# The later modulation sums without a seed page: the bias is added where the sums are used

## The chip, the cores and the metric

One core of a Trainium2 chip runs one transformer block in a single launch. The time is the device time of an execution in microseconds (us), as the median of several. The core's engines are TensorE (PE in the profile, with its weight loads as PEld), VectorE (DVE), ScalarE (ACT), GpSimd (POOL) and SyncE (SP). Each has an instruction queue of its own; SP's queue issues nearly all DMA transfers.

## The reference, cut to what matters

```python
mod = jax.nn.silu(c) @ w_mod[layer] + b_mod[layer]            # 1 x 12288
sh_m, sc_m, g_m, sh_f, sc_f, g_f = jnp.split(mod[:, None, :], 6, axis=-1)
h_lat = rms_norm(x, nw[0]) * (1.0 + sc_m) + sh_m              # and the same for 256 context tokens
m_ctx, m_lat = hybrid_mixer(h_ctx, h_lat, ...)                # gated LRU and gated delta net, w_in, w_out
x = x + g_m * rms_norm(m_lat, nw[1])
h = rms_norm(x, nw[2]) * (1.0 + sc_f) + sh_f
x = x + g_f * rms_norm(sq_relu_mlp(h, w_ff1, w_ff2), nw[3])
```

The model has 2048 columns, 512 tokens (and 256 context tokens), and an inner width of 8192 in the last product. The modulation `mod` has six chunks of 2048 columns: 0 and 1 are needed at the start, 2 (`g_m`) behind the mixer, 3 and 4 (`sh_f`, `sc_f`) ahead of the last product, and 5 (`g_f`) at the very end. Everything is 32-bit; the large products are made of pairs of rounded pieces (high times high, high times low, low times high), so each weight piece is split into a high part `wh` (a cast on ScalarE) and a low part `wl` (a subtraction on VectorE or GpSimd, `split`, line 67 and 61) before TensorE multiplies it.

## The kernel before, in words

The program runs in stages. First comes the modulation's chunks 0 and 1, by matmuls. Then the mix stage: the product with `w_in`, and between its tiles the tasks of the mixer, which a planner in the source hands out in slots. Then the product with `w_out` (`project`), and then the last product, block by block: `ff1(b)` multiplies by a 512-column block of `w_ff1` (16 weight pieces), `ff2(b)` by the matching rows of `w_ff2` (four quarters of four pieces, with four additions on VectorE behind each quarter). The order is ff1_half for blocks 0 and 1, ff2(0), ff1(2), ff2(1), ff1(3), ff2(2), ff1(4), and so on. Three buffers each hold raw weights (`wr`), high parts and low parts, so that about three pieces are split ahead of TensorE.

Chunks 2 to 5 of the modulation are running sums. `modacc` (line 1144) takes one quarter of a chunk, 512 columns: it loads sixteen 128 x 512 slices of `w_mod` into the five pages of the tag `ld` and accumulates each on VectorE, times one column of silu(c) (`stt`, line 64). Partition p then holds the sum over sixteen of the 2048 rows, and a matmul with a matrix of ones later adds the partitions up. The bias enters through a seed: a page of the tag `macc`, which has one buffer, is cleared on GpSimd (line 1148), the bias row is loaded into its partition 0 (line 1149), and the first accumulate adds this page. In chunks 2 to 4 the sum itself is kept in a PSUM bank and copied to the seed page at the end (line 1164); in chunk 5 the seed page is the sum. The page is stored to `accD` in memory (line 1165).

The sums are read back where they are used: `gm_rows` (chunk 2, line 1292) and `modrow` (chunk 5, line 1181) multiply by the ones matrix to have the row on all partitions; `mod_vecs` (chunks 3 and 4, line 1308) makes columns of it. The call of chunk 5 stands in the source behind ff2(2): sixty-four accumulates, and then `modrow`'s four matmuls ahead of ff1(4). Its accumulates carry a manual order edge to an earlier VectorE instruction (`after`).

A scheduler in the framework gives each engine its final queue at compile time. It takes instructions in the order of the source as a priority, but an instruction may go far ahead of that place if its inputs and its buffer are there. Buffers of one tag are handed out in the order of the source. Pages of the common tag (`pg`) are a pool of 29; tags such as `macc` and `ld` have buffers of their own.

The two strict triangle masks GT and LT are made on GpSimd (line 77) and copied to rounded forms GTr and LTr on ScalarE (lines 89 and 90).

Of the kernel before, what the change touches and what calls it, by code (L numbers as in the profile page):

```python
# [7 lines left out]
F32 = mybir.dt.float32  # L8
# [3 lines left out]
ALU = mybir.AluOpType  # L12
# [4 lines left out]
P = 128  # L17
# [14 lines left out]
def build(tc, A, out, stop=None, dump=None):  # L32
# [3 lines left out]
    with es:  # L36
        cp = es.enter_context(tc.tile_pool(name="const", bufs=1))
        wp = es.enter_context(tc.tile_pool(name="weights", bufs=2))
        pp = es.enter_context(tc.tile_pool(name="pages", bufs=29))
        ld_n = 5  # L40

        pg = ps = es.enter_context(tc.tile_pool(name="psum", bufs=8, space=PSUM))
# [7 lines left out]
        def page(dt=F32, tag="pg", shape=(P, 512), bufs=None):  # L50
            kw = {} if bufs is None else {"bufs": bufs}
            return pp.tile(list(shape), dt, tag=tag, name=nm(tag), **kw)
# [22 lines left out]
        def select(name, op, mult, patt, dt=F32):  # L75
            t = const([P, P], dt, name)
            G.affine_select(out=t, in_=ones, compare_op=op, fill=0.0, base=0,
                            pattern=[[patt, P]], channel_multiplier=mult)
            return t
# [2 lines left out]
                        pattern=[[-1, P]], channel_multiplier=1)  # L82
        LE = select("LE", ALU.is_ge, -1, 1)
        GE = select("GE", ALU.is_ge, 1, -1)
        GT = select("GT", ALU.is_gt, 1, -1)
        LT = select("LT", ALU.is_gt, -1, 1)
        GTr = const([P, P], F32R, "GTr")
        LTr = const([P, P], F32R, "LTr")
        S.copy(GTr, GT)
        S.copy(LTr, LT)  # L90
        sel = const([4, 2], F32, "sel")
        G.affine_select(out=sel, in_=ones[:4, :2], compare_op=ALU.is_ge, fill=0.0, base=0,
                        pattern=[[-2, 2]], channel_multiplier=1)
# [1050 lines left out]
        def modacc(chunk, f, after=None):  # L1144

            col = chunk * D + f * 512
            acc = seed = page(tag="macc", bufs=1)
            G.memset(acc, 0.0)
            SP.dma_start(acc[0:1, :], A["b_mod"][:, col:col + 512])
            if after is None:  # L1150
                acc = bank()
            q = []
            for k in range(17):
                if k < 16:
                    w = page(tag="ld", bufs=ld_n)
                    SP.dma_start(w, wmod[:, k, col:col + 512])
                    q.append(w)
                if k > 0:
                    stt(acc, q.pop(0), silc[:, k - 1:k], seed if k == 1 else acc, ALU.mult, ALU.add)
                    if after is not None:  # L1160
                        tc.add_manual_dep(nc.cur_bb.bb.instructions[-1], after, NOSYNC, reason="order")
                    yield 0.7, 0, 0
            if after is None:
                S.copy(seed, acc)
            SP.dma_start(accD[4 * (chunk - 2) + f], seed)
            modok.add((chunk, f))

        def modload(chunk, f):
            a = page(tag="ld", bufs=ld_n)
# [3 lines left out]
        def modrow(chunk, nrow):  # L1173

            res = []
            for f in range(4):
                a = modload(chunk, f)
                nb = page(tag="ld", bufs=ld_n)
                SP.dma_start(nb, A["norm_w"][0, nrow:nrow + 1, f * 512:(f + 1) * 512].to_broadcast([P, 512]))
                b = bank()  # L1180
                T.matmul(b, ones, a, start=True, stop=True)
                g = page()
                tt(V, g, b, nb, ALU.mult)
                res.append(g)
            return res

        def modcol(chunk, dst):
            for f in range(4):
                a = modload(chunk, f)
                b = bank()  # L1190
                for i in range(4):
                    T.matmul(b[:, i:i + 1], a[:, i * P:(i + 1) * P], ones[:, 0:1], start=True, stop=True)
                V.tensor_copy(dst[:, 4 * f:4 * f + 4], b[:, 0:4])


        ORD = "ckcccucc cccccFzc ccculuyu uycuuymu Lgxggggg ggggggyg yzxgyggg xxgyyxxg gggxggzx zzzzz".replace(" ", "")
# [86 lines left out]
        def gm_rows():  # L1283
            while any((2, f) not in modok for f in range(4)):
                yield 0, 0, 1
            for f in range(4):
                a = modload(2, f)
                nb = page(tag="ld", bufs=ld_n)
                SP.dma_start(nb, A["norm_w"][0, 1:2, f * 512:(f + 1) * 512].to_broadcast([P, 512]))
                yield 0, 0, 2  # L1290
                b = bank()
                T.matmul(b, ones, a, start=True, stop=True)
                g = page()
                tt(V, g, b, nb, ALU.mult)
                gm.append(g)
                yield 0.6, 0, 0
# [3 lines left out]
        def mod_vecs():  # L1300
            for ch, dst in ((3, shf), (4, scf)):
                while any((ch, f) not in modok for f in range(4)):
                    yield 0, 0, 1
                a = [modload(ch, f) for f in range(4)]
                yield 0, 0, 2
                b = bank()
                for i in range(16):
                    T.matmul(b[:, i:i + 1], a[i // 4][:, i % 4 * P:i % 4 * P + P], ones[:, 0:1], start=True, stop=True)
                V.tensor_copy(dst, b[:, 0:16])
                del a  # L1310
            stt(scf, scf, 1.0, nw2, ALU.add, ALU.mult)
            colok.append(1)
            yield 0.1, 0, 0
# [280 lines left out]
```

## Time and profile before

| | us |
|---|---|
| runs before (median of 3) | 2782.72 (2778.91 to 2784.66) |
| the profiled execution, its own time | 2792.65 |
| its span, first to last instruction | 2790.9 |
| TensorE busy | 2661.4 (95%) |
| VectorE busy | 1676.4 (60%) |
| ScalarE busy | 1183.7 (42%) |
| GpSimd busy | 585.0 (21%) |

In the profile, a row of a group gives the line, the engine, the operation, the tiles it writes and reads and the count, then the busy time and the mean of one in nanoseconds, then the idle time of the engine right before these instructions with what ended it. A row of the timeline gives the start, the duration and in brackets the idle time before it with its releaser. A row of the waits gives who waited for whom, the sum in us, how often, and the longest. A DMA row gives the size and the median time from issue to landing. Matmuls overlap in the pipeline, so a step from one start to the next says more of their pace than one duration.

### The profile page before, as it was taken

The numbers are of one execution on the slowest core, as the hardware profiler recorded it, in microseconds if no ns is written. First come the engines' busy times: TensorE is split into PE (matmuls) and PEld (weight loads), VectorE is DVE, ScalarE is ACT, GpSimd is POOL, SyncE is SP. The second block draws the span as 40 slices with busy tenths as digits, with TensorE's granted clock in tenths as the row PEclk, the third lists the DMA queues.
The fourth block names the chain that finished last, engine by engine and source line by source line (L and its number), as shares of the span: only waits on it lengthen the run. The fifth ranks groups of instructions, "written<-read, shape, count | busy, mean of one in ns | idle before, by whom it ended". The sixth has DMA issues, their size and how long they took to land.

```text
span 2790.9 us, 39585 instructions
## 1 busy us (share of the span) xinstructions
PE 2661.4 (95%) x14253; PEld 2181.3 (78%) x14253; DVE 1676.4 (60%) x3287; ACT 1183.7 (42%) x2418; POOL 585.0 (21%) x552
## 2 busy tenths in 40 slices
PE   7989999899999998978999999999999999999998
PEld 2478797677877787866898887888888888888886
DVE  6785757877797785857588443344343443434436
ACT  5555577545556654535552222222222222222223
POOL 0145354434344434326300000000000000000002
PEclk9989999999999998989999999999999999999999
DMA  9654475556666676646788333333233333333334
GB/s 355 208 164 127 115 202 166 161 168 198 194 197 193 185 216 216 195 143 205 231 268 276 113 94 118 99 98 98 93 97 98 98 98 97 95 97 98 98 99 155
DMA packets 374968, 434.33 MB, mean 156 GB/s; under 512 B 22665, under 2 KB 212450, under 8 KB 374770
## 3 DMA queue, kind: packets, MB, share of 16 engines
q1 hardware_dynamic: 374160, 431.66, 49.7%
q8 instruction: 112, 1.84, 0.3%
q14 instruction: 86, 0.70, 0.1%
q10 hardware_dynamic: 610, 0.13, 0.0%
HBM read 401.31 MB, written 30.41 MB: 155 GB/s over the span
## 4 chain that ended last, share of the span: by engine, by line
PE 69%; DVE 8%; issue 3%; DMA 2%; ACT 2%; POOL 1%; SPq 0%; DVEq 0%; ACTq 0%; POOLq 0%
PE bk L1510 8%; PE bk L1509 8%; PE bk L1508 8%; PE bk L1498 7%; PE bk L1499 7%; PE bk L1497 7%; PE bk L523 3%; PE bk L525 3%; PE bk L524 3%; PE bk L1419 2%; PE bk L1420 2%; PE bk L1418 2%; DVE pg L64 2%; DVE bk L64 1%; DVE pg L61 1%
## 5 line engine op out<-in xcount | busy, mean ns | idle before, releaser
L67 ACT CAST wh<-wr 128x512 fp32r<-128x512 f32 x952 | 583.4, 618 | 1212.8 <-PE bk L1498 446.6
L61 DVE TENSOR_TENSOR wl<-wr,wh 128x512 fp32r<-128x512 f32 x642 | 463.2, 723 | 776.3 <-ACT wh L67 661.0
L61 POOL TENSOR_TENSOR wl<-wr,wh 128x512 fp32r<-128x512 f32 (+1 forms) x310 | 400.9, 1300 | 587.1 <-ACT wh L67 522.8
L1510 PE MATMUL bk<-wl,pg 128*128 128x512 f32 x960 | 374.0, 390 | 0.5 <-DVE wl L61 0.5
L1509 PE MATMUL bk<-wh,pg 128*128 128x512 f32 x960 | 373.9, 390 | 0.0
L1508 PE MATMUL bk<-wh,pg 128*128 128x512 f32 x960 | 373.9, 389 | 0.0
L1497 PE MATMUL bk<-H2h,wh 128*128 128x512 f32 x896 | 349.4, 390 | 0.0
L1498 PE MATMUL bk<-H2l,wh 128*128 128x512 f32 x896 | 349.0, 389 | 0.0
L1499 PE MATMUL bk<-H2h,wl 128*128 128x512 f32 x896 | 349.0, 389 | 0.0
L523 PE MATMUL bk<-Hlh,wh 128*128 128x512 f32 (+1 forms) x784 | 316.1, 403 | 5.4 <-ACT wh L67 5.4
L525 PE MATMUL bk<-Hlh,wl 128*128 128x512 f32 (+1 forms) x784 | 311.4, 397 | 7.6 <-POOL wl L61 7.4
L524 PE MATMUL bk<-Hll,wh 128*128 128x512 f32 (+1 forms) x784 | 309.8, 395 | 0.0
L61 POOL TENSOR_TENSOR big<-big,pg 128x512 f32<-128x512 f32 x9 | 12.0, 1342 | 1245.6 <-ACT pg L1570 1245.6
L1510 PEld LDWEIGHTS bk<-wl,pg 128*128 128x128 f32 x960 | 180.2, 188 | 38.1 <-DVE wl L61 0.9
L1508 PEld LDWEIGHTS bk<-wh,pg 128*128 128x128 f32 x960 | 180.3, 188 | 37.4
L1509 PEld LDWEIGHTS bk<-wh,pg 128*128 128x128 f32 x960 | 180.3, 188 | 37.3
L1497 PEld LDWEIGHTS bk<-H2h,wh 128*128 128x128 f32 x896 | 168.3, 188 | 35.1 <-issue 0.2
L1498 PEld LDWEIGHTS bk<-H2l,wh 128*128 128x128 f32 x896 | 168.3, 188 | 35.1 <-issue 0.2
L1499 PEld LDWEIGHTS bk<-H2h,wl 128*128 128x128 f32 x896 | 168.2, 188 | 34.8
L525 PEld LDWEIGHTS bk<-Hlh,wl 128*128 128x128 f32 (+1 forms) x784 | 148.2, 189 | 45.5 <-POOL wl L61 13.0
L523 PEld LDWEIGHTS bk<-Hlh,wh 128*128 128x128 f32 (+1 forms) x784 | 148.7, 190 | 36.6 <-ACT wh L67 6.6
L524 PEld LDWEIGHTS bk<-Hll,wh 128*128 128x128 f32 (+1 forms) x784 | 148.6, 190 | 29.7
(348 smaller groups left out, 4524.9 us busy)
## 6 DMA issues: line engine op xcount, KB each, us to landing
wr<-in_w_ff SPq DMA_DIRECT2D x272, 512.0 KB, 4.1
wr<-in_w_in SPq DMA_DIRECT2D x144, 512.0 KB, 4.0
ld<-in_w_mod SPq DMA_DIRECT2D x256, 256.0 KB, 4.0
mr<-in_w_mod SPq DMA_DIRECT2D x32, 1024.0 KB, 11.0
wr<-in_w_out SPq DMA_DIRECT2D x64, 512.0 KB, 4.6
pg<-vkD SPq DMA_DIRECT2D x88, 128.0 KB, 4.1
ld<-in_x SPq DMA_DIRECT2D x32, 256.0 KB, 4.8
vkD<-pg SPq DMA_DIRECT2D x24, 256.0 KB
```

Of the source, the lines that this page charges most:

```text
L61: e.tensor_tensor(out=out, in0=a, in1=b, op=op)
L64: V.scalar_tensor_tensor(out=out, in0=a, scalar=s, in1=b, op0=op0, op1=op1)
L67: S.copy(hi, src)
L523: T.matmul(pt[:m, :n], wh, a, start=k == 0, stop=False)
L524: T.matmul(pt[:m, :n], wh, b, start=False, stop=False)
L525: T.matmul(pt[:m, :n], wl, a, start=False, stop=k == 15)
L1497: T.matmul(bk[c], w[kk][0][:, s_], hh, start=k == 0, stop=False)
L1498: T.matmul(bk[c], w[kk][0][:, s_], hl_, start=False, stop=False)
L1499: T.matmul(bk[c], w[kk][1][:, s_], hh, start=False, stop=k == 15)
L1508: T.matmul(o, ah, h, start=k == 0, stop=False)
L1509: T.matmul(o, al, h, start=False, stop=False)
L1510: T.matmul(o, ah, l, start=False, stop=k == 3)
```

## The change

The seed page is gone, and with it its memset, its bias load and the tag `macc`. The first accumulate becomes a plain multiplication by a scalar. The sum is in a PSUM bank as before for chunks 2 to 4 and copied to a page of the common tag; for chunk 5 it is a page of the common tag from the start. The common pool has 30 pages instead of 29.

The bias is added at the use. For chunks 2 and 5, `modbias` loads the bias row into one partition of an `ld` page, and `modsum` adds a second matmul of one row (ones times the bias row) to the same bank. For chunks 3 and 4, the copy out of PSUM becomes an addition of the bias columns that the kernel keeps from its start. The masks GTr and LTr are now one minus the other triangles, made on VectorE, and GT and LT are the same tiles read as plain 32-bit. A function without a caller, `modcol`, is dropped.

```diff
-        pp = es.enter_context(tc.tile_pool(name="pages", bufs=29))
+        pp = es.enter_context(tc.tile_pool(name="pages", bufs=30))
...
-        GT = select("GT", ALU.is_gt, 1, -1)
-        LT = select("LT", ALU.is_gt, -1, 1)
...
-        S.copy(GTr, GT)
-        S.copy(LTr, LT)
+        for m, mr in ((LE, GTr), (GE, LTr)):
+            V.tensor_scalar(out=mr, in0=m, scalar1=-1.0, scalar2=1.0, op0=ALU.mult, op1=ALU.add)
+        GT, LT = GTr.bitcast(F32), LTr.bitcast(F32)
...
         def modacc(chunk, f, after=None):
             col = chunk * D + f * 512
-            acc = seed = page(tag="macc", bufs=1)
-            G.memset(acc, 0.0)
-            SP.dma_start(acc[0:1, :], A["b_mod"][:, col:col + 512])
-            if after is None:
-                acc = bank()
+            acc = page() if after is not None else bank()
...
-                    stt(acc, q.pop(0), silc[:, k - 1:k], seed if k == 1 else acc, ALU.mult, ALU.add)
+                    if k == 1:
+                        V.tensor_scalar_mul(acc, q.pop(0), silc[:, 0:1])
+                    else:
+                        stt(acc, q.pop(0), silc[:, k - 1:k], acc, ALU.mult, ALU.add)
...
             if after is None:
-                S.copy(seed, acc)
-            SP.dma_start(accD[4 * (chunk - 2) + f], seed)
+                acc, w = page(), acc
+                S.copy(acc, w)
+            SP.dma_start(accD[4 * (chunk - 2) + f], acc)
...
+        def modbias(chunk, f):
+            r = page(tag="ld", bufs=ld_n)[0:1, :]
+            SP.dma_start(r, A["b_mod"][:, chunk * D + f * 512:chunk * D + f * 512 + 512])
+            return r
+
+        def modsum(b, a, r):
+            T.matmul(b, ones, a, start=True, stop=False)
+            T.matmul(b, ones[0:1, :], r, start=False, stop=True)
...
-                a = modload(chunk, f)
+                a, r = modload(chunk, f), modbias(chunk, f)
...
-                T.matmul(b, ones, a, start=True, stop=True)
+                modsum(b, a, r)
...
-                V.tensor_copy(dst, b[:, 0:16])
+                tt(V, dst, b[:, 0:16], bmod[:, 16 * ch:16 * ch + 16], ALU.add)
```

The change moves instructions of chunk 5. On VectorE before, its 64 accumulates (`macc`) stand among the splits of ff1_half and ff2(0), from row 2019 of VectorE's queue to row 2160. Here is the end of the last quarter, with the splits `wl` of ff2(0) and ff1(2) around it:

```order
L61 TENSOR_TENSOR wl_16233<-wr_16226,wh_16232 128x512
L64 SCALAR_TENSOR_TENSOR macc_17492<-ld_17527,silc,macc_17492 128x512
L64 SCALAR_TENSOR_TENSOR macc_17492<-ld_17530,silc,macc_17492 128x512
L64 SCALAR_TENSOR_TENSOR macc_17492<-ld_17533,silc,macc_17492 128x512
L61 TENSOR_TENSOR wl_16263<-wr_16260,wh_16262 128x512
L64 SCALAR_TENSOR_TENSOR macc_17492<-ld_17536,silc,macc_17492 128x512
L64 SCALAR_TENSOR_TENSOR macc_17492<-ld_17539,silc,macc_17492 128x512
L61 TENSOR_TENSOR wl_16267<-wr_16260,wh_16266 128x512
L61 TENSOR_TENSOR wl_16297<-wr_16294,wh_16296 128x512
```

The additions of ff2(2) and of `modrow` follow a hundred rows behind, from row 2262 on.

On VectorE now, the accumulates (`pg_17320`, `pg_17370`, `pg_17420`, `pg_17470`, one page for each quarter) begin at row 2172, within the first quarter of ff2(2), and 26 of them stand there between splits and additions. This is the end of ff2(2) (`big` and `S` are its last additions), the start of what follows:

```order
L61 TENSOR_TENSOR wl_17575<-wr_17568,wh_17574 128x512
L61 TENSOR_TENSOR big_15791<-big_15791,bk_17244 128x512
L61 TENSOR_TENSOR big_15793<-big_15793,bk_17245 128x512
L61 TENSOR_TENSOR big_15795<-big_15795,bk_17246 128x512
L61 TENSOR_TENSOR S_15799<-S_15799,bk_17247 128x512
L64 SCALAR_TENSOR_TENSOR pg_17370<-ld_17400,silc,pg_17370 128x512
L61 TENSOR_TENSOR wl_17605<-wr_17602,wh_17604 128x512
L64 SCALAR_TENSOR_TENSOR pg_17370<-ld_17403,silc,pg_17370 128x512
L64 SCALAR_TENSOR_TENSOR pg_17370<-ld_17406,silc,pg_17370 128x512
```

Behind the split `wl_17605` (the third of ff1(4)) 37 accumulates stand in one block, rows 2229 to 2265 of the queue; then come `modrow`'s four additions and only then the next split.

On TensorE the place of chunk 5 is the same in both. Before it has four rows (line 1181) between the last row of ff2(2) (line 1510) and the first of ff1(4) (line 1497). Now (all lines behind the masks' are one or more off):

```order
L1511 MATMUL bk_17247<-wl_17289,pg_16402 128x512
L1174 MATMUL bk_17526<-ld_17520,ones 128x512
L1175 MATMUL bk_17526<-ld_17522,ones 128x512
L1174 MATMUL bk_17537<-ld_17531,ones 128x512
L1175 MATMUL bk_17537<-ld_17533,ones 128x512
L1174 MATMUL bk_17548<-ld_17542,ones 128x512
L1175 MATMUL bk_17548<-ld_17544,ones 128x512
L1174 MATMUL bk_17559<-ld_17553,ones 128x512
L1175 MATMUL bk_17559<-ld_17555,ones 128x512
L1498 MATMUL bk_17564<-H2h_13478,wh_17570 128x512
```

Each of the four matmuls has its one-row matmul for the bias behind it; nothing else moved there. On SP, the loads of `w_mod` for chunk 5 moved with the accumulates, behind the weight loads of ff2(2), and each of the four reads of `accD` has a bias load and a load of `norm_w` beside it. On GpSimd the sixteen memsets are gone and the order of the rest is the same, but for a few rows that changed places with a neighbour. The accumulates of chunks 2 to 4 stand where they stood.

More of the change, by code (lines that the diff above doesn't have):

```diff
@@ L1185, in modrow @@
             return res
[L1187 to L1193, printed above, removed]
         ORD = "ckcccucc cccccFzc ccculuyu uycuuymu Lgxggggg ggggggyg yzxgyggg xxgyyxxg gggxggzx zzzzz".replace(" ", "")
@@ L1286, in gm_rows @@
             for f in range(4):
-                a = modload(2, f)
+                a, r = modload(2, f), modbias(2, f)
                 nb = page(tag="ld", bufs=ld_n)
@@ L1291, in gm_rows @@
                 b = bank()
-                T.matmul(b, ones, a, start=True, stop=True)
+                modsum(b, a, r)
                 g = page()
```

## The prediction

> **What bounds the kernel now.** I read the page first: its engine table, then the waits of TensorE (PE), then the windows around the places that the diff touches (a window row has the stretch, its length, the busy time of PE, PE's weight loads, DVE, ACT and POOL with their instructions, the granted clock, the DMA share, GB/s).
>
> ```profile
> span 2790.9 us, 39585 instructions
> PE 2661.4 (95%) x14253; PEld 2181.3 (78%) x14253; DVE 1676.4 (60%) x3287; ACT 1183.7 (42%) x2418; POOL 585.0 (21%) x552
> 390.00:1300.00 910.00, 846.02 (x5177) 701.09 (x5176) 676.72 (x1486) 503.27 (x1144) 384.67 (x367) 0.96 0.62 189
> 1424.00:1535.00 111.00, 109.08 (x634) 96.32 (x634) 94.02 (x151) 37.96 (x71) 1.58 (x3) 1.00 0.86 284
> ```
>
> TensorE sets the end: 95% busy. A microsecond counts only where it reaches TensorE's queue. Two stretches matter. From 390 to 1300 us, where chunks 2 to 4 of the modulation are summed, TensorE idles 910.0 - its busy time of 846.0 = 64 us. From 1424 to 1535, where chunk 5 is summed today, it idles 1.9 us only, though VectorE (DVE) is busy for 94 of 111 us and the DMA engines for 86%: chunk 5 costs nothing there.
>
> **The change part by part.** The largest part is not an operation but a place. Today chunk 5's running sums write a page of their own tag, so they could be put far ahead of their use. Now they take pages of the common pool, and the order rows shown with the change have them 150 DVE rows later, around ff2(2): 27 of the 64 accumulates stand between the additions of ff2(2) or right behind the last of them, then one weight split, and then 37 in one block without a split between. On TensorE nothing moved: the ones-matmuls of chunk 5 still stand between ff2(2) and ff1(4), and its queue runs in order. So TensorE must stop there until the 37 are done. Today it passes that place like this:
>
> ```profile
> 1684.57 2.74 PE L1181 MATMUL bk<-ld,ones 128*128 128x512 f32 x6
> 1689.93 1.12 PE L1181 MATMUL bk<-ld,ones 128*128 128x512 f32 x2 [2.62 <-DMA ld<-accD]
> 1690.49 0.80 PE L1497 MATMUL bk<-H2h,wh 128*128 128x512 f32 x1
> ```
>
> Call T the start of that place, 1684.6. ff1(4) resumes some 6.4 us after it (1691.0: the two instructions of the last call take 1.1).
>
> First, do the 27 accumulates inside ff2(2) slow TensorE? The new order puts eight of them into each quarter of ff2(2). Today's ff2(0) already has just that mix:
>
> ```profile
> 1487.25 1.88 DVE L1514 COPY big<-bk 128x512 f32<-128x512 f32 x3
> ...
> 1490.24 2.32 DVE L64 SCALAR_TENSOR_TENSOR macc<-ld,silc,macc 128x512 f32<-128x512 f32 x3
> 1492.48 0.68 DVE L61 TENSOR_TENSOR wl<-wr,wh 128x512 fp32r<-128x512 f32 x1
> 1493.08 2.33 DVE L64 SCALAR_TENSOR_TENSOR macc<-ld,silc,macc 128x512 f32<-128x512 f32 x3
> 1495.32 0.69 DVE L61 TENSOR_TENSOR wl<-wr,wh 128x512 fp32r<-128x512 f32 x1
> 1495.92 1.53 DVE L64 SCALAR_TENSOR_TENSOR macc<-ld,silc,macc 128x512 f32<-128x512 f32 x2
> ...
> 1498.13 1.88 DVE L1514 COPY big<-bk 128x512 f32<-128x512 f32 x3
> ...
> 1488.70 0.62 ACT L67 CAST wh<-wr 128x512 fp32r<-128x512 f32 x1 [2.10 <-PE bk L1509]
> 1491.42 0.62 ACT L67 CAST wh<-wr 128x512 fp32r<-128x512 f32 x1 [2.10 <-PE bk L1509]
> ```
>
> Eight accumulates between two groups of additions 10.88 us apart, and ScalarE's (ACT) casts, which follow TensorE, keep 2.72 us, the pace of twelve matmuls. So: no cost until T.
>
> Then the block of 37. Its pace has two bounds. Three in a row take 2.32 us and each lasts about 0.75, so a step is (2.32 - 0.75)/2 = 0.785 us: 37 take 29.0 us if the loads keep up. The other bound is a stretch in which they did not, since the accumulates share five load pages:
>
> ```profile
> 1519.13 0.75 DVE L64 SCALAR_TENSOR_TENSOR macc<-ld,silc,macc 128x512 f32<-128x512 f32 x1 [0.30 <-DMA ld<-in_w_mod]
> ...
> 1525.62 0.75 DVE L64 SCALAR_TENSOR_TENSOR macc<-ld,silc,macc 128x512 f32<-128x512 f32 x1 [0.42 <-DMA ld<-in_w_mod]
> ...
> 1532.02 0.75 DVE L64 SCALAR_TENSOR_TENSOR macc<-ld,silc,macc 128x512 f32<-128x512 f32 x1 [1.55 <-DMA ld<-in_w_mod]
> ld<-in_w_mod SPq DMA_DIRECT2D x256, 256.0 KB, 4.0
> accD<-macc SPq DMA_DIRECT2D x16, 256.0 KB, 2.0
> ld<-accD SPq DMA_DIRECT2D x16, 256.0 KB, 4.0
> ld<-in_norm_w SPq DMA_DIRECT2D x8, 256.0 KB, 3.8
> ```
>
> These three are five accumulates apart each, (1532.02 - 1519.13)/10 = 1.29 us a step, with weight loads in between that the block will not have. Without them a page goes round in 4.0 (load to landing) + 0.75 (accumulate) + about 0.5 (issue on SP, a bit over the 0.25 to 0.49 of the SP rows below) = 5.25 us, by five pages 1.05 us. I take 1.05 after the first five, which lie loaded: 5 x 0.785 + 32 x 1.05 = 37.5 us. The bounds stay 29.0 (all at 0.785) and 45.2 (32 at 1.29).
>
> By the Trainium skill, "DMA: Bandwidth & Descriptors", section "Anatomy of one DMA", a transfer takes about 2.0 us and its bytes at 436 GB/s, 2.6 us for 256 KB; a page would then go round in under 0.785 us a step and VectorE alone would set the pace, 29.0 us. The row's 4.0 us speaks against it; the page's fit is for another issuing engine, and the row decides.
>
> ```profile
> 1684.88 0.68 DVE L61 TENSOR_TENSOR S<-S,bk 128x512 f32<-128x512 f32 x1
> ```
>
> Today the last addition of ff2(2) ends 1.0 us after T; with an accumulate and a split behind it (0.75 and 0.6 apart) the block starts at T + 2.3. Behind it: the last sum is stored (2.0), read back (4.0), and two matmul calls follow (0.9 each by the 2.74 us for six instructions, two to a call); that is 7.8, at least 8 with issue. But the four slices now need three load pages each of five, twelve in all, so the last two slices' loads wait for the first ones' matmuls and additions: two load times in a row (3.8 + 4.0) and the matmuls, up to 13. I take 10. So ff1(4) resumes at T + 2.3 + 37.5 + 10 = T + 49.8, where it was T + 6.4: **+43.4 us**. The splits for its first three weight pieces (8.2 us of TensorE work) are done by then, which covers those that come next.
>
> A long stop also costs clock. This is the pace after a wait of 6.35 us:
>
> ```profile
> 1066.52 0.79 PE L1418 MATMUL bk<-wh,M 128*128 128x512 f32 x1 [6.35 <-ACT M L67]
> ...
> 1070.22 0.63 PE L1419 MATMUL bk<-wh,M 128*128 128x512 f32 x1
> 1070.65 0.61 PE L1420 MATMUL bk<-wl,M 128*128 128x512 f32 x1
> ...
> 1073.34 0.39 PE L1418 MATMUL bk<-wh,M 128*128 128x512 f32 x1
> 1073.56 0.39 PE L1419 MATMUL bk<-wh,M 128*128 128x512 f32 x1
> ```
>
> Steps of 0.43 instead of 0.22 us, for about 4.5 us: half of that is lost, **+2**, bounds 0 and 4.
>
> By the Trainium skill, "TensorE: Matmul & The Clock Gate", section "Part 1: The HAM clock gate", the array runs at half clock until some 3.4 us of activity; half of that is 1.7 us. The rows agree, with about 4.5 us at the half pace; by the page the term would be 1.7.
>
> What the mix stage (390 to 1300) gains: twelve memsets, each behind the store of the sum before, leave GpSimd's (POOL) in-order queue, and twelve bias loads leave SP's.
>
> ```profile
> 520.83 0.52 POOL L1148 MEMSET macc<- 128x512 f32 x1 [11.34 <-ACT bk L593]
> 522.64 0.79 PE L525 MATMUL bk<-Hlh,wl 128*128 128x512 f32 x1 [2.54 <-POOL wl L61]
> 1059.36 0.99 SPq L1109 DMA_DIRECT2D prodD<-pg  x2
> 1062.77 0.25 SPq L1149 DMA_DIRECT2D macc<-in_b_mod  x1
> 1063.07 0.39 SPq L1369 DMA_DIRECT2D ld<-prodD  x1
> PE bk L525 <- POOL wl L61: 15.6, 19, 2.5
> POOL macc L1148 <- DMA accD<-macc: 103.0, 11, 35.6
> DVE bk L64 <- DMA macc<-in_b_mod: 11.9, 4, 7.0
> ```
>
> One memset held the splits behind it until TensorE idled 2.5 us; one bias load held SP for 2.4 us (1060.35 to 1062.77) ahead of the load on which TensorE's 6.35 us hang. That is 4.9 in sight, and some of it is given back at the stage's serial end: **-4**. The bounds are 0 and -15.6, all that TensorE ever waited for GpSimd's splits there. The 11.9 us that VectorE waited for bias rows reached TensorE nowhere that I can see.
>
> The rest: four added one-row matmuls for chunk 2 stand in TensorE's busy stretch, at 0.9 at most 3.4, less where the stage's end has slack: **+2**; their bias rows take load pages there and may delay SP, which the upper bound of +6 takes in. The 1.9 us of 1424 to 1535 may come back: **-1**. The add with the bias columns in place of two 16-column copies, two masks on VectorE in place of two on GpSimd and two casts at the load-bound start, and the first accumulates as plain multiplies: nothing, under other work. The 30th page itself changes no order that I can find on TensorE.
>
> Sum: 43.4 + 2 - 4 + 2 - 1 = **+42.4**. The profiled execution took 2792.65 us (span 2790.9), so it would be 2835.1; the median of the runs shown lies 9.9 lower, 2782.72, and I predict for that: **2825**.
>
> **The rivals.**
> - *VectorE paces the block* (29.0 for 37.5): 2817. For it: the block runs without weight loads beside it. Against: the 4.0 us row.
> - *The loads are as slow as at 1519 to 1532* (45.2): 2833. For it: two stores of sums fall into the block. Against: no 512 KB weight loads there.
> - *The mix stage gives back more than the block costs.* Each memset held GpSimd (103 us of waiting on stores in all) and so the splits. It decides if more than 42 of TensorE's 64 idle us return; with all of them 2782.7 - 64 + 46 = 2765. Against: its waits for GpSimd sum to 15.6, most without a memset before them.
> - *The change doesn't move the wait*: VectorE has a good part of the 37 done before T after all, or TensorE's stop is short because the sums of the last slices come early. Then only the small terms are left, 2782.7 - 3 = 2780. Against: both queues run in the order shown, and the eight per quarter are what fits at TensorE's pace.
>
> **How the numbers follow.** The forecast 0.72, VectorE's pace 0.10, slow loads 0.10, the mix stage 0.04, no moved wait 0.04. Low end: 2.3 + 29.0 + 8 - 6.4 = 32.9, with no clock loss and -12 from the mix: +21, 2804. High end: 2.3 + 45.2 + 13 - 6.4 = 54.1, +4, +6: +64, 2847. All between is slower. Within 0.2% (5.6 us, about what can be told from no change) only the last rival falls, faster only the mix rival and a part of the last: faster 0.05, same 0.03, slower 0.92.
>
> **What would show it.** In the new profile: one TensorE wait of 30 to 50 us for a load of accD or the bias row, between the last ff2(2) and the first ff1(4) matmul near 1680; in the 40 slices a dip there, with the DMA rate up in the same slices and down at 1424 to 1535; in the block VectorE waiting for w_mod loads about 0.3 us per accumulate (none: VectorE's pace); clock under 1.0 for a slice after it; no memset on GpSimd and less of TensorE's waiting for its splits. I am wrong if TensorE crosses that place in under 15 us, or if the mix stage ends over 15 us earlier or later than now.

## The result and the profile after

The changed kernel takes 2828.24 us (median, 2827.57 to 2830.47), the kernel before 2781.77 beside it: a ratio of 1.0153, 95% interval 1.0131 to 1.0174. A second comparison gave 2829.54 against 2787.74, 1.0147 (1.0116 to 1.0178). So the change costs 41.8 to 46.5 us; 2825 had been predicted, within 2804 to 2847. The profiled execution took 2828.55 us.

First the page of the changed kernel: its span, the engine table, and of the 40 slices (70.7 us each) TensorE's busy tenths, its granted clock and the DMA rate.

```profile
span 2826.8 us, 39598 instructions
PE 2675.6 (95%) x14269; PEld 2183.2 (77%) x14269; DVE 1672.1 (59%) x3289; ACT 1185.3 (42%) x2416; POOL 572.7 (20%) x534
PE   7988999899999989979999968999999999999998
PEclk9999999999999998989999987999999999999999
GB/s 357 202 167 126 122 207 161 160 190 193 203 212 169 211 214 205 202 150 185 243 157 97 97 253 149 97 97 97 97 97 97 97 97 97 96 98 97 97 98 153
```

The 24th slice (1625 to 1696 us) shows TensorE at six tenths and the DMA engines at 253 GB/s. The granted clock falls in the 24th and 25th, to 0.8 and 0.7. That is the place predicted, and the waits of TensorE name it:

```profile
PE bk L1174 <- DMA ld<-accD: 36.0, 1, 36.0
PE bk L524 <- POOL wl L61: 10.8, 15, 1.1
```

One wait of 36.0 us is new; TensorE's waits for GpSimd's splits fell from 15.6 to 10.8. Now TensorE's timeline there. T, the end of ff2(2), is 1708.59 - 36.04 = 1672.55.

```profile
1708.59 2.07 PE L1174 MATMUL bk<-ld,ones 128*128 128x512 f32 x2 [36.04 <-DMA ld<-accD]
1710.60 2.07 PE L1175 MATMUL bk<-ld,ones 1*128 1x512 f32 x2
1712.60 2.08 PE L1174 MATMUL bk<-ld,ones 128*128 128x512 f32 x2
1714.60 2.07 PE L1175 MATMUL bk<-ld,ones 1*128 1x512 f32 x2
...
1722.62 2.07 PE L1175 MATMUL bk<-ld,ones 1*128 1x512 f32 x2
1724.62 0.80 PE L1498 MATMUL bk<-H2h,wh 128*128 128x512 f32 x1
```

TensorE stops for 36.0 us, then needs 16.0 us for eight calls of 2.0 us each, and ff1(4) starts at T + 52.1. VectorE's and SP's timelines of the same stretch:

```profile
1673.96 0.69 DVE L61 TENSOR_TENSOR wl<-wr,wh 128x512 fp32r<-128x512 f32 x1
1674.57 3.90 DVE L64 SCALAR_TENSOR_TENSOR pg<-ld,silc,pg 128x512 f32<-128x512 f32 x5
...
1689.33 3.90 DVE L64 SCALAR_TENSOR_TENSOR pg<-ld,silc,pg 128x512 f32<-128x512 f32 x5 [0.61 <-DMA ld<-in_w_mod]
...
1705.56 3.11 DVE L64 SCALAR_TENSOR_TENSOR pg<-ld,silc,pg 128x512 f32<-128x512 f32 x4 [0.62 <-DMA ld<-in_w_mod]
```

```profile
1693.64 10.87 SPq L1151 DMA_DIRECT2D ld<-in_w_mod  x12
1704.96 0.33 SPq L1179 DMA_DIRECT2D ld<-accD  x1
...
1708.70 0.33 SPq L1164 DMA_DIRECT2D accD<-pg  x1
...
1716.70 0.33 SPq L1179 DMA_DIRECT2D ld<-accD  x1
```

The block of 37 accumulates runs from 1674.57 to 1708.67, 34.1 us, and waits for loads in between. SP could issue the first read-back only behind the last load of `w_mod`, at 1704.96; its landing ends TensorE's wait. The last sum is stored at 1708.70 and read back from 1716.70 on, while TensorE still works on the calls ahead.

Last the two stretches shown of before, in the same columns as there:

```profile
390.00:1300.00 910.00, 856.39 (x5215) 708.19 (x5214) 675.13 (x1499) 508.71 (x1150) 378.71 (x357) 0.96 0.63 191
1424.00:1535.00 111.00, 111.00 (x612) 97.23 (x611) 50.36 (x84) 36.69 (x67) 0.00 (x0) 1.00 0.40 124
```

From 390 to 1300 TensorE idles 53.6 us instead of 64.0. From 1424 to 1535, where chunk 5 is gone, it idles no more.

One table of all kernels follows, worked out from TensorE's timelines of the profiled executions; the medians beside it are of all runs. What each kernel changes is told with its experiment. "Mix 1" runs from the span's start to the matmul behind the long wait for ScalarE's product (1066.52 before; in ld6 this wait is 2.44 us only), "mix 2" from there to the first transpose behind the wait of 7.28 us (1227.60 before), "to T" from there to the end of ff2(2), "place" from T to the first matmul of ff1(4), "rest" to the span's end. In row_later nothing stands at the place; its calls come in "rest".

| kernel | mix 1 | mix 2 | to T | place | rest | median |
|---|---|---|---|---|---|---|
| before | 1066.5 | 161.1 | 457.0 | 5.9 | 1100.4 | 2781.8 |
| before_again | 1071.2 | 156.2 | 456.2 | 5.8 | 1100.2 | 2787.4 |
| pool_only | 1065.0 | 155.7 | 454.1 | 46.8 | 1100.2 | 2825.6 |
| after | 1055.7 | 162.9 | 453.9 | 52.1 | 1102.2 | 2828.2 |
| after_again | 1059.1 | 161.4 | 454.3 | 53.3 | 1102.9 | 2829.5 |
| own_tag | 1055.7 | 160.4 | 460.8 | 12.8 | 1102.3 | 2797.4 |
| no_bias_row | 1057.8 | 160.4 | 452.8 | 46.6 | 1101.3 | 2819.1 |
| full_rows | 1057.1 | 153.8 | 453.7 | 47.4 | 1100.7 | 2814.7 |
| own_tag_vec | 1058.2 | 156.4 | 461.1 | 9.1 | 1101.1 | 2788.8 |
| gm_fold | 1060.9 | 151.1 | 453.1 | 53.6 | 1102.5 | 2822.1 |
| fold | 1056.8 | 151.1 | 460.0 | 6.1 | 1100.6 | 2778.4 |
| fold2 | 1052.3 | 148.4 | 457.4 | 5.9 | 1102.9 | 2775.7 |
| row_later | 1057.7 | 164.2 | 453.7 | 0 | 1127.9 | 2802.6 |
| ld6 | 1053.0 | 163.2 | 453.7 | 48.3 | 1104.3 | 2822.7 |

The kernel before alone gave medians from 2781.8 to 2788.6 in the five comparisons; each ratio below is to the runs of before beside it. Single executions of one kernel differ by some us in the mix stage, so a difference there is read from several rows.

### The profile page after: what moved, and what is told of

Its sections match the earlier page's. It is cut to its first block, busy times and chain, and to the rows that moved or that the text cites. A ratio compares the mean times of both kernels' runs of the same rounds, so it can differ in the third digit from the quotient of the medians.

```text
span 2826.8 us, 39598 instructions
## 1 busy us (share of the span) xinstructions
PE 2675.6 (95%) x14269; PEld 2183.2 (77%) x14269; DVE 1672.1 (59%) x3289; ACT 1185.3 (42%) x2416; POOL 572.7 (20%) x534
## 4 chain that ended last, share of the span: by engine, by line
PE 51%; DVE 2%; DMA 1%; POOL 0%; ACT 0%; issue 0%; DVEq 0%; SPq 0%; ACTq 0%; POOLq 0%
PE bk L1511 8%; PE bk L1510 8%; PE bk L1509 8%; PE bk L1498 7%; PE bk L1500 7%; PE bk L1499 7%; PE bk L1470 1%; PE bk L1469 1%; PE bk L1468 1%; PE bk L1421 1%; PE bk L1420 1%; PE bk L1419 1%; DMA ld<-in_w_mod 1%; DMA wr<-in_w_ff 1%; DVE pg L64 0%; DVE wl L61 0%
## 5 line engine op out<-in xcount | busy, mean ns | idle before, releaser
L1509 PEld LDWEIGHTS bk<-wh,pg 128*128 128x128 f32 x960 | 180.3, 188 | 37.3
L522 PEld LDWEIGHTS bk<-Hlh,wh 128*128 128x128 f32 (+1 forms) x784 | 148.4, 189 | 34.0 <-ACT wh L67 4.2
```

Source lines behind the costliest of these rows:

```text
L522: T.matmul(pt[:m, :n], wh, a, start=k == 0, stop=False)
L1509: T.matmul(o, ah, h, start=k == 0, stop=False)
```

## The experiments

**The same two kernels again.** No edit.

> The kernel before, unchanged, for a second profile. The first profile took 2792.65 us, ten more than the median 2781.8, so shares of the change read off two profiles are uncertain by that much. If the ten us are a property of that one execution, this one takes 2779 to 2785 us and TensorE reaches the four chunk-5 ones-matmuls some 10 us before 1684.6, near 1674; then the mix stage gained little from the change (TensorE reaches that place at 1672.5 in the changed kernel). If profiled executions are simply slower, it takes about 2792 and the gain of the mix stage is real (9 to 12 us).

> The changed kernel, unchanged, timed beside the other experiments, since the kernel before moved from 2781.8 us (4 runs) to 2787.4 (14 runs) between two comparisons. If the stop of TensorE is all that counts and the rest is scatter of single executions, it takes 2828 to 2833 us; its profile shows again a wait of 36 us for the load of accD, 16 us of eight half-clock calls behind it, and TensorE at that place within 4 us of 1672.5.

Measured: 2787.35 against 2787.37 (1.0003, 0.9991 to 1.0015), and T at 1683.7 again. So the first profile was not an outlier, and T comes 9 to 12 us earlier in the changed kernel. The changed kernel again: 2829.54, a wait of 37.3 us and the same eight calls of 2.0 us, T at 1674.8.

**The place alone (pool_only).** In the kernel before, chunk 5's sums go to common pages; seed, bias and matmuls stay.

```diff
-            if after is None:
-                acc = bank()
+            acc = bank() if after is None else page()
...
+            else:
+                seed = acc
```

> The kernel before (29 pages, seed page with the bias, one matmul per slice), but chunk 5's running sums write common pages from their first accumulate on. Its 37 accumulates stand in one block behind ff2(2) as in the changed kernel. Theory (the place costs): TensorE reaches the place at T and stops 36 us, then four matmul calls, the last one waiting for store and read-back: it resumes about T + 44.3 instead of T + 6.4, +38 us: 2820 us, 2812 to 2828. Rival (something else in the change costs): 2779 to 2787, as before.

Measured: 2825.58 (2820.75 to 2832.11), ratio 1.0147 (1.0124 to 1.0169). The waits of TensorE and its timeline at the place:

```profile
PE bk L1182 <- DMA ld<-accD: 41.2, 3, 39.9
1714.73 2.07 PE L1182 MATMUL bk<-ld,ones 128*128 128x512 f32 x2 [39.94 <-DMA ld<-accD]
1717.03 2.96 PE L1182 MATMUL bk<-ld,ones 128*128 128x512 f32 x4 [0.23 <-DMA ld<-accD]
1720.99 1.13 PE L1182 MATMUL bk<-ld,ones 128*128 128x512 f32 x2 [1.00 <-DMA ld<-accD]
```

These lines alone bring 38 us (2825.58 against 2787.37), the ratio of the whole change, with the seed page still there: the place takes 46.8 us instead of 5.9. VectorE again has 37 accumulates in a row behind ff2(2). The tail behind the wait is short here, 6.8 us for four calls, and the clock rises within it (2.07 us for two instructions, then 1.13).

**The place undone (own_tag).** In the changed kernel, chunk 5's sums write a page of their own tag again.

```diff
-        pp = es.enter_context(tc.tile_pool(name="pages", bufs=30))
+        pp = es.enter_context(tc.tile_pool(name="pages", bufs=29))
...
-            acc = page() if after is not None else bank()
+            acc = page(tag="macc", bufs=1) if after is not None else bank()
```

> The changed kernel, but chunk 5's running sums write a page of their own tag again (one buffer, and 29 common pages), so that its accumulates stand where they did, 2019 to 2159 in VectorE's order. Everything else of the change stays: no seed, bias at the use, 12 loads before the four calls. Theory (the place costs): the 36 us stop of TensorE is gone, what is left is the 8 matmuls instead of 4 and their twelve loads (+3 to +8 us at that place) and the gain of the mix stage (-2 to -12): 2780 us, 2768 to 2790. Rival (the added matmuls, the bias loads or the changed page count cost): 2810 to 2828 still.

Measured: 2797.41 (2793.7 to 2799.82), ratio 1.0039 (1.0024 to 1.0055). The stop is gone, which settles the cause of some 30 us, but 10 us stay, and neither theory had them. TensorE at the place, and two windows of it, with the clock in the column behind the five engines:

```profile
1676.89 1.02 PE L1174 MATMUL bk<-ld,ones 128*128 128x512 f32 x2
1677.84 1.12 PE L1175 MATMUL bk<-ld,ones 1*128 1x512 f32 x2
...
1682.50 1.30 PE L1174 MATMUL bk<-ld,ones 128*128 128x512 f32 x2 [1.43 <-DMA ld<-accD]
1683.73 2.07 PE L1175 MATMUL bk<-ld,ones 1*128 1x512 f32 x2
...
1689.73 0.80 PE L1498 MATMUL bk<-H2h,wh 128*128 128x512 f32 x1
1679.91:1683.32 3.41, 1.98 (x5) 0.59 (x4) 0.69 (x1) 0.00 (x0) 0.00 (x0) 1.00 0.87 228
1683.33:1686.70 3.37, 3.37 (x4) 1.00 (x4) 0.69 (x1) 0.00 (x0) 0.00 (x0) 0.50 0.31 109
```

A wait of only 1.43 us among these calls, and the clock falls to 0.50: the last three calls take 2.07 us instead of 1.12, and ff1(4) begins slowly. The place costs 12.8 us where it cost 5.9. The table has the rest: against before_again, 4.6 us more to T, 4.1 in mix 2 and 2.1 behind the place, and 15.5 less in mix 1. (The profiled execution is own_tag's fastest, 2793.7 us, so these rows do not show all of the 10 us.) In the kernel before, four full-row calls had kept the clock, with the wait of 2.62 us among them:

```profile
1685.51:1688.92 3.41, 1.80 (x5) 0.49 (x3) 1.94 (x4) 0.00 (x0) 0.00 (x0) 1.00 0.57 204
1688.93:1692.33 3.40, 2.40 (x9) 1.67 (x10) 1.39 (x2) 0.00 (x0) 0.00 (x0) 1.00 0.95 315
```

Hence a new theory: calls with one row do not keep the clock up. no_bias_row, run beside own_tag, and three further kernels bear on it.

**Tail without the one-row calls (no_bias_row, full_rows).** From the changed kernel; no_bias_row leaves the bias of chunk 5 out, full_rows leaves that of chunks 2 and 5 out and counts the sums twice:

```diff
 no_bias_row, chunk 5:
-                modsum(b, a, r)
+                T.matmul(b, ones, a, start=True, stop=True)
 full_rows, chunks 2 and 5:
-            T.matmul(b, ones[0:1, :], r, start=False, stop=True)
+            T.matmul(b, ones, a, start=False, stop=True)
```

> The changed kernel, but chunk 5's rows are summed by one matmul per slice: the bias row of that chunk is neither loaded nor added, which leaves this part of the computation out. In the changed kernel TensorE is busy for the 16.0 us from the end of its 36 us wait to ff1(4), eight calls of 2.0 us each at half clock. Theory (half clock sets the tail): with four calls of 2.0 and the last slice's store and read-back TensorE resumes near T + 44.3 instead of T + 52.1: 2820 us, 2816 to 2823, with a new wait of TensorE of 2 to 5 us for the last load. Rival (load pages and latency set the tail, as predicted): the matmuls leave and TensorE waits in their place, 2826 to 2829.

> The changed kernel, but the second matmul of each call (chunk 2 and chunk 5) multiplies the page of the sum again (128 rows) instead of the one-row bias, which is loaded all the same: the bias of these rows is left out and the sum counted twice. Same number of calls, pages and loads. With one-row calls in between the clock stayed at 0.50 for all 16.0 us of the tail; without them (no_bias_row) it rose to 1.00 some 3.5 us after TensorE resumed. Theory (one-row matmuls don't count as activity for the clock): the clock rises 3 to 5 us into the tail, which takes 9 to 12 us instead of 16.0: 2822 us, 2818 to 2826, by the before of 2782 to 2787. Rival (the clock stays low because these calls come after a long stop or in four passes): 16 us again, the time of after_again within 2 us.

Measured: no_bias_row 2819.11, ratio 1.0118 (1.0094 to 1.0142); full_rows 2814.73, ratio 1.0102 (1.0074 to 1.013). The clock of no_bias_row behind its stop, and the tail of full_rows:

```profile
1709.60:1713.00 3.40, 3.40 (x4) 1.10 (x4) 0.69 (x1) 0.00 (x0) 0.00 (x0) 0.51 0.74 268
1713.00:1715.30 2.30, 1.35 (x3) 0.30 (x2) 0.69 (x1) 0.00 (x0) 0.00 (x0) 1.00 0.67 173
```

```profile
1701.55 2.08 PE L1174 MATMUL bk<-ld,ones 128*128 128x512 f32 x2 [36.89 <-DMA ld<-accD]
1703.42 1.91 PE L1175 MATMUL bk<-ld,ones 128*128 128x512 f32 x2
1705.12 1.23 PE L1174 MATMUL bk<-ld,ones 128*128 128x512 f32 x2
1706.19 1.02 PE L1175 MATMUL bk<-ld,ones 128*128 128x512 f32 x2
```

With full rows alone the clock is back after 3.4 us (no_bias_row) and 3.9 us (full_rows, at 1705.46); eight calls then take 10.5 us (1701.55 to 1712.08), where the same eight, every second one with one row, took 16.0 at 0.50 to the end. So one-row calls held the clock down. The tail of no_bias_row was not quite as expected: instead of one wait of 2 to 5 us there are two, 0.95 for a read-back and 1.20 for VectorE, and behind them the clock is at 0.50 once more (1716.36 to 1719.78), so ff1(4) starts at T + 46.6 and not 44.3. full_rows came out 7 us under what was expected of it, and the table shows where: mix 2 takes 153.8 instead of 160 to 163. The four one-row calls of chunk 2 stand there.

**Chunk 2's one-row calls (gm_fold).** In the changed kernel, VectorE adds chunk 2's bias row to partition 0 of the finished sum, and each of its rows is one matmul again.

```diff
+                elif chunk == 2:
+                    r = modbias(chunk, f)
...
+            if r is not None:
+                tt(V, acc[0:1, :], acc[0:1, :], r, ALU.add)
...
-                modsum(b, a, r)
+                T.matmul(b, ones, a, start=True, stop=True)
```

> The changed kernel, but chunk 2's bias row is added to partition 0 of the finished sum by VectorE (1 x 512), as in fold, so that the four one-row matmuls in the mix stage are gone; chunk 5 is as in the changed kernel, with its 37 accumulates behind ff2(2). In the changed kernel the first of these one-row matmuls stands at 1066, 10 us behind a 7.28 us wait, and the granted clock of 1060 to 1080 is 0.67 to 0.76; 21.8 us pass between the first and the second call, where full_rows has 15.4 with a clock of 0.91. Theory (one-row calls so near to a wait keep the clock low): 6 to 8 us less in the mix stage and the same 36 to 37 us stop: 2822 us, 2818 to 2825. Rival (these calls cost only their own 3.4 us, or are covered): 2826 to 2831.

Measured: 2822.14 (2820.67 to 2826.24), ratio 1.0122 (1.0105 to 1.0139), 6.1 and 7.4 us under the two medians of the changed kernel, with the stop unchanged at 37.6 us. Mix 2 takes 151.1. The window from 1060 to 1080, first of the changed kernel, then of full_rows:

```profile
1060.00:1080.00 20.00, 20.00 (x221) 15.85 (x220) 5.56 (x14) 7.03 (x16) 7.80 (x9) 0.67 0.48 159
```

```profile
1060.00:1080.00 20.00, 20.00 (x275) 16.21 (x274) 7.28 (x18) 9.90 (x21) 9.60 (x11) 0.91 0.67 203
```

TensorE is busy for all 20 us in both, but at a clock of 0.67 it works on 221 instructions instead of 275. A busy column alone does not show this loss. Narrower windows show a stretch at 0.50 that begins 2 to 4.5 us behind the first one-row call (1066.86 in the changed kernel), 1069.20 to 1082.85 there. It lasts 10.24 or 13.65 us in all six kernels with these calls (after, after_again, own_tag, no_bias_row, row_later, ld6); the five without them (full_rows, own_tag_vec, gm_fold, fold, fold2) have none, or 3.41 us in gm_fold. One-row calls are not the only way to lose the clock there: the first profile of the kernel before has 13.65 us of it too, behind a wait of 2.30 us for a load of accD at 1079.19, where before_again and pool_only have 3.41; that makes most of the 5 us by which their mix 2 is shorter.

**The bias on VectorE (own_tag_vec).** own_tag, with the bias loaded to all partitions and added by VectorE, chunks 2 and 5 (the broadcast load and own_tag's two lines are not shown).

```diff
-            T.matmul(b, ones, a, start=True, stop=False)
-            T.matmul(b, ones[0:1, :], r, start=False, stop=True)
+            T.matmul(b, ones, a, start=True, stop=True)
...
-                tt(V, g, b, nb, ALU.mult)
+                tt(V, g, b, r, ALU.add)
+                tt(V, g, g, nb, ALU.mult)
```

> As own_tag (chunk 5's sums in a page of their own tag, 29 common pages), and the bias is no longer added by a one-row matmul: a broadcast load brings it to all partitions and VectorE adds it to the bank, for chunk 2 and chunk 5. own_tag took 2797.4 us; at the place of chunk 5's rows its TensorE spent 12.8 us (8 calls, the last three at 2.0 us, clock 0.50) where the kernel before spent 6.4. Theory (the one-row matmuls let the clock fall): four calls at 0.9, clock 1.00 throughout, 6 to 8 us at the place: 2789 us, 2783 to 2793. Rival (the clock falls by the idle time alone, or the loss lies elsewhere): clock 0.50 again behind the wait, 2795 to 2800.

Measured: 2788.75 (2783.19 to 2791.88), ratio 1.0006 (0.999 to 1.0021), as expected in time, but not all for the reason given. The place takes 9.1 us, and the clock fell there too:

```profile
1681.17 2.08 PE L1174 MATMUL bk<-ld,ones 128*128 128x512 f32 x2 [3.61 <-DMA ld<-accD]
1679.80:1681.80 2.00, 0.63 (x1) 0.50 (x2) 0.69 (x1) 0.00 (x0) 0.00 (x0) 0.60 1.04 331
```

Each slice needs three load pages, as in own_tag, and the third slice's sum lands 5.5 us behind T (5.6 in own_tag). With two calls instead of four ahead of it, the wait is 3.61 us instead of 1.43, and that is enough without a one-row call. The place is 3.7 us shorter than own_tag's; most of the rest of the gain is in mix 2 (156.4 for 160.4).

**The rows later (row_later).** The changed kernel with `modrow` two blocks later.

```diff
+            if b == 5:
                 gf = modrow(5, 3)
```

> The changed kernel (sums in common pages), but the four rows of chunk 5 are read back and summed two feed-forward blocks later, behind ff2(4) instead of behind ff2(2). Of the 37 accumulates that stood in one block, 24 now stand between weight splits of ff1(4), one to five at a time, and the last 12 in a row. Theory (TensorE stopped only because its in-order queue met the ones-matmuls before the sums were there): no wait of TensorE for a load of accD over 3 us; left are the eight calls (13 to 16 us instead of 6.4) and up to 6 us for the 12 accumulates in a row ahead of a split: 2793 us, 2786 to 2802. Rival (the accumulates cost TensorE wherever they stand beside the feed-forward blocks, through VectorE or the loads): 2808 to 2828.

Measured: 2802.56 (2799.95 to 2806.09), ratio 1.0053 (1.0036 to 1.0071), just above the range. The wait for accD is down to 1.36 us, but the twelve accumulates in a row hold the splits behind them for longer than the pieces ahead last:

```profile
1719.43 0.80 PE L1498 MATMUL bk<-H2h,wh 128*128 128x512 f32 x1 [11.11 <-ACT wh L67]
```

That wait and the slow matmuls behind it make ff1(4) 56.6 us long, where a block without a wait takes 43.5; the eight calls take 12.1 us at their new place (1862.67 to 1874.79), the last two at 2.0 us each, and ff1(6) 46.1. So the stop does come from TensorE meeting the calls too early, and an uninterrupted run of accumulates costs in either place. The term "up to 6 us" was too small: 11.1.

**The pace of the block (ld6).** The changed kernel with six load pages, and one common page less.

```diff
-        pp = es.enter_context(tc.tile_pool(name="pages", bufs=30))
-        ld_n = 5
+        pp = es.enter_context(tc.tile_pool(name="pages", bufs=29))
+        ld_n = 6
```

> The changed kernel with six load pages instead of five (and 29 common pages instead of 30). In the changed kernel the last 37 accumulates took 34.1 us, 0.92 each, with VectorE waiting for w_mod loads in between and the DMA engines at 86%, 289 GB/s. Theory (a page goes round in 4.6 us and five pages set the pace, as predicted): six pages give 0.77, so VectorE's own 0.785 sets it: the accumulates behind ff2(2) take 28 to 29.5 us, the stop of TensorE falls to about 31 us, the time to 2824 us (2820 to 2828). Rival (the DMA engines' throughput sets the pace): still 0.90 to 0.93 each, 36 to 37 us of stop, 2827 to 2833.

Measured: 2822.68 (2820.24 to 2827.3), ratio 1.0124 (1.011 to 1.0139); the stop is 32.3 us. VectorE in the block:

```profile
1672.10 0.75 DVE L64 SCALAR_TENSOR_TENSOR pg<-ld,silc,pg 128x512 f32<-128x512 f32 x1
...
1681.31 6.26 DVE L64 SCALAR_TENSOR_TENSOR pg<-ld,silc,pg 128x512 f32<-128x512 f32 x8 [0.36 <-DMA ld<-in_w_mod]
...
1692.69 6.26 DVE L64 SCALAR_TENSOR_TENSOR pg<-ld,silc,pg 128x512 f32<-128x512 f32 x8 [2.00 <-DMA ld<-in_w_mod]
1699.16 3.17 DVE L64 SCALAR_TENSOR_TENSOR pg<-ld,silc,pg 128x512 f32<-128x512 f32 x4 [0.21 <-DMA ld<-in_w_mod]
```

And a window of the block, first of the changed kernel, then of ld6 (the last two columns are the busy share of the DMA engines and their GB/s):

```profile
1674.57:1708.60 34.03, 0.01 (x1) 0.01 (x1) 27.03 (x38) 0.00 (x0) 0.00 (x0) 0.53 0.86 284
```

```profile
1674.00:1704.00 30.00, 1.82 (x2) 0.50 (x2) 24.39 (x34) 0.00 (x0) 0.00 (x0) 0.50 0.89 299
```

Eight in a row now run at 0.79. The 35 accumulates behind ff2(2) (1672.10 to 1702.33, less two splits of 0.6) take 0.83 each instead of 0.92. So the pages set the pace of 0.92, as the sixth shortens it; but 0.77 to 0.785 was expected, and waits for loads stay, with the DMA engines at 299 GB/s and 89% busy. What sets the pace with six pages was not tried.

**A version that beats both (fold, fold2).** own_tag, with the bias of chunks 2 and 5 added as in gm_fold; fold2 has two pages for chunk 5's sums and 28 common ones. The main lines of fold's edit:

```diff
-        pp = es.enter_context(tc.tile_pool(name="pages", bufs=30))
+        pp = es.enter_context(tc.tile_pool(name="pages", bufs=29))
...
-            acc = page() if after is not None else bank()
+            acc = page(tag="macc", bufs=1) if after is not None else bank()
...
+                elif chunk in (2, 5):
+                    r = modbias(chunk, f)
...
+            if r is not None:
+                tt(V, acc[0:1, :], acc[0:1, :], r, ALU.add)
...
-                modsum(b, a, r)
+                T.matmul(b, ones, a, start=True, stop=True)
```

> A version meant to beat both: chunk 5's sums in a page of their own tag (29 common pages), no seed, no one-row matmul: for chunks 2 and 5 VectorE adds the bias row to partition 0 of the finished sum (1 x 512) before it is stored, so each row is again one matmul. Chunks 3 and 4 as in the changed kernel. Theory: the mix stage keeps the 10 us that the missing memsets give by 1041 us and does not lose them to the clock behind the first one-row call (TensorE leaves the mix stage 11 to 15 us earlier than in before_again, as in own_tag_vec and full_rows); the place of chunk 5's rows is back at 6.4 us; ff2(0) still costs 0 to 3 us: 2777 us, 2770 to 2784. Rival (what the mix stage gains is given back at its serial end whatever the bias does): 2784 to 2790.

> As fold, with two pages for chunk 5's running sums (28 common pages), so that a slice's first accumulate does not wait for the store of the slice before (2.15 us of VectorE, and loads queued behind it, in own_tag). Theory (the single page costs TensorE the waits for splits in ff2(0)): 1 to 3 us under fold: 2775 us, 2768 to 2783. Rival (hidden, or one common page less costs): within 2 us of fold or above it.

Measured: fold 2778.42 (2774.23 to 2782.36), ratio 0.9966 (0.9953 to 0.9979); fold2 2775.66 (2768.86 to 2779.34), ratio 0.9951 (0.9937 to 0.9965). TensorE of fold at the place:

```profile
1667.94 2.74 PE L1192 MATMUL bk<-ld,ones 128*128 128x512 f32 x6
1673.51 1.13 PE L1192 MATMUL bk<-ld,ones 128*128 128x512 f32 x2 [2.83 <-DMA ld<-accD]
1674.07 0.79 PE L1500 MATMUL bk<-H2h,wh 128*128 128x512 f32 x1
```

The place is back at 6.1 us, and the gain of the mix stage stays: TensorE leaves it at 1208.0, 19.5 us earlier than in before_again, where 11 to 15 had been expected. Both ratios lie below 1 with their intervals, so the gain of 0.3 to 0.5% on the kernel before is clear of the noise. Between the two the table shows 460.0 and 457.4 to T, as expected of a second page, but their intervals overlap: that fold2 is the faster one is not shown.

## Why the prediction was right

*The place.* Right, and shown by pool_only (the place alone brings 38 us) and own_tag (without it 2797.4). In the terms of the prediction:

| step | predicted | measured |
|---|---|---|
| accumulates inside ff2(2) | 0 | 0: ff2(2) takes 43.5 us before, 43.7 after |
| block starts | T + 2.3 | T + 2.0 (1674.57) |
| 37 accumulates | 37.5 (29.0 to 45.2) | 34.1 |
| tail | 10 (8 to 13) | 16.0 |
| ff1(4) resumes, against before | +43.4 (49.8 less 6.4) | 52.1 and 53.3, less 5.9 and 5.8: +46 to +47 |
| clock behind it | +2 | ff1(4) takes 45.2 and 45.7, was 44.0: +1.2 to +1.7 |
| mix stage | -4 | -10.4 (mix 1) |
| one-row calls of chunk 2 | +2, up to 6 | +4.2 (mix 2); 6.1 to 7.4 by gm_fold |
| 1424 to 1535 | -1 | -2.5 (to T, both kernels twice) |

The mix rows are the mean of the five kernels with the change's mix stage and five load pages (after, after_again, own_tag, no_bias_row, row_later) against the three with that of before (before, before_again, pool_only). The first profile of before weighs on mix 2: against the other two alone it is +5.9. The 6.4 us that the prediction takes off run to the end of the last call of the kernel before; ff1(4) starts at T + 5.9 there.

*The block.* The mechanism (five pages go round) held, by ld6. A round took 34.1/37 x 5 = 4.6 us, not the 5.25 added up from load, accumulate and issue.

*The tail.* This step failed in its reason, and 16.0 us lie beyond its bound of 13. It was made of store, read-back and load pages, with 0.9 us for each call at full clock. Those latencies were hidden: TensorE did not wait once in 16.0 us. What set the tail were the eight calls at half clock. The prediction had seen that a long stop costs clock, but put it behind the tail only, and took from the row at 1066 that it returns in 4.5 us whatever runs.

*The mix stage.* A gain was right, its size and reason were not. The wait near 1066, where a bias load was to give 2.4 us back, grew from 6.35 to 7.28 us. The gain lies ahead of it. pool_only, which keeps the seed page, has none of it (1065.0), so it comes with the edits around the seed or the masks; the memsets left GpSimd's queue there, but which edit brings it was not tried alone. The one-row calls were priced at their own 3.4 us at most, with a bound of 6 for their loads; the clock they hold down costs more.

*The sum.* The measured terms add up to about +39, and so do the profiles (mean span of after and after_again 2828.9, of before and before_again 2790.3: +38.6); the medians differ by 41.8 and 46.5, as both profiled executions of before were slower than their medians. The predicted +42.4 is that near because its errors cancel: the tail came out 6 us longer and the one-row calls dearer, the block 3.4 shorter and the mix stage 6.4 better. The stop itself was foreseen; that the number hit so closely was luck.

*The rivals.* Not VectorE's pace (it waited for loads, 0.92 us a step instead of 0.785), not loads as slow as 1.29 us a step, no mix stage that gives back 42 us, and the wait did move.

## What to carry to other kernels

A buffer's tag decides where a scheduler may put the work that writes it: here, taking the sums from a pool that is handed out in source order moved 64 accumulates from a stretch where they cost TensorE nothing to right ahead of their use, and TensorE, which runs its queue in order, stopped for 36 us. Read the order of the queues before pricing the operations. Add a bias row on an engine that has time, into one partition of the sum, rather than with a one-row matmul, as fold does: in these runs the price of that matmul was less its own time than the clock around it.

## What the runs showed of the hardware

One-row matmuls did not bring the clock back. Behind a stop of 36 to 39 us, full-row calls alone had it at 1.00 after 3.4 us (no_bias_row) and 3.9 us (full_rows); every second call with one row kept it at 0.50 for all 16.0 us. By the Trainium skill, "TensorE: Matmul & The Clock Gate", section "Part 1: The HAM clock gate", some 3.4 us of activity open the gate; the full-row kernels agree, the one-row calls do not, though TensorE was busy throughout.

What makes it fall can be read from narrower windows. In these traces the clock is 1.00 or 0.50, and between the first and the last matmul a stretch at 0.50 lasts 3.41 us or a multiple of it: one in fold2 (1664.26 to 1667.68), three in own_tag (1683.32 to 1693.56). So the 3.41 us ahead of each fall can be set beside the like stretch, on the same grid, of the kernels that kept the clock at the place. These are the two of fold2 and of no_bias_row:

```profile
1660.85:1664.26 3.41, 0.85 (x3) 0.49 (x3) 0.85 (x2) 0.00 (x0) 0.00 (x0) 1.00 0.91 250
1664.27:1667.67 3.40, 3.40 (x9) 2.52 (x8) 0.69 (x1) 0.00 (x0) 0.00 (x0) 0.50 0.81 272
1712.95:1716.36 3.41, 1.40 (x3) 0.30 (x2) 1.30 (x2) 0.00 (x0) 0.00 (x0) 1.00 0.74 218
1716.37:1719.77 3.40, 3.28 (x6) 1.97 (x7) 0.76 (x2) 0.00 (x0) 0.00 (x0) 0.50 0.80 240
```

| kernel | stretch of 3.41 us | TensorE busy | of it with full rows | clock behind it |
|---|---|---|---|---|
| own_tag_vec | from 1676.80 | 0.75 | 0.75 | 0.50 |
| fold2 | from 1660.85 | 0.85 | 0.85 | 0.50 |
| no_bias_row | from 1712.95 | 1.40 | 1.40 | 0.50 |
| own_tag | from 1679.91 | 1.98 | 0.86 | 0.50 |
| row_later | from 1866.36 | 2.05 | 1.05 | 0.50 |
| before | from 1685.51 | 1.80 | 1.80 | 1.00 |
| before_again | from 1687.39 | 1.83 | 1.83 | 1.00 |
| fold | from 1672.05 | 1.95 | 1.95 | 1.00 |

With full rows for 1.80 us or more the clock stayed; with 1.40 or less it fell. own_tag and row_later were busy for longer than the three that kept it, and lost it: the one-row calls did not count there either, though the waits among them were only 1.43 and 1.36 us. It also shows why a wait of 2.62 us cost nothing in the kernel before and a stretch at half clock in fold2: before, 1.61 us of it fell on one stretch and 1.01 on the next; in fold2 nearly all of it, 2.56 us, fell on one.

The same reading holds for every stretch from 1400 to 2750 us in all fourteen traces, where little but large products runs beside these calls. The clock fell 15 times, behind 1.40 us of full rows or less, and was kept with 1.73 us or more. It rose 15 times, behind 3.19 us or more, and stayed at 0.50 with 2.80 us or less; in the tails, where every second call has one row, the full rows fill at most 2.01 us of a stretch until the dense matmuls return. Only no run was made to vary this share, so what it has to be between 1.40 and 1.73 us, and between 2.80 and 3.19, stays open.
